# RWKV state chains in three slots a chunk, filter norms summed on TensorE, and operands of filters and convolutions prepared one unit ahead

## The chip, the core and the metric

One core of a Trainium2 chip. The metric is the device time of one execution in microseconds (us), as the median of several runs. Engines: TensorE (PE, its weight loads PEld), VectorE (DVE), ScalarE (ACT), GpSimd (POOL), and SyncE (SP), which issues most DMAs.

## The reference

A two-layer diffusion network over 1024 latent and 256 context tokens. The even layer is the one that matters here. Half of its channels go through RWKV-7 time mixing in both directions (8 heads of 64), the other 512 through an order-2 Hyena long convolution with implicit filters; both are projected from the same input and their outputs meet in one output projection. Then follow a mixture of experts, an attention layer and a second mixture.

```python
def step(s, inp):                      # RWKV, one token
    r_t, w_t, k_t, v_t, kk_t, a_t = inp
    sa = jnp.einsum('bhij,bhj->bhi', s, kk_t)
    s = s * w_t[:, :, None, :] - sa[..., None] * (kk_t * a_t)[:, :, None, :] + v_t[..., None] * k_t[:, :, None, :]
    return s, jnp.einsum('bhij,bhj->bhi', s, r_t)
...
norm = jnp.sum(jnp.abs(fwd), axis=0) + jnp.sum(jnp.abs(bwd), axis=0) + 1e-6
kc = jnp.concatenate([fwd, jnp.zeros((1, HY_ORDER, HY_WIDTH), f32), bwd], axis=0) / norm
...
z = x1 * (fft_long_conv(v, kf[:, 0]) + v * hy_b[0])
return x2 * (fft_long_conv(z, kf[:, 1]) + z * hy_b[1])
```

## The kernel before, in words

The RWKV recurrence is computed in chunks of 32 tokens, 40 steps in sequence, both directions and all heads at once; two chunks form a window whose operands are loaded together (`rw_chain`, line 873 on). A step multiplies the state S with the chunk's rows (line 914), subtracts the part from within the chunk (pA, line 900) to give the right side rh, multiplies with the inverse T of the chunk's triangular system (line 920), copies the result from PSUM into uv, next to v, which a DMA has put there (lines 890 and 926), multiplies uv with the decayed keys bt (line 932) and adds the decayed old state pr, which GpSimd makes. The outputs pY (lines 939 and 940) come from uv and the old state. The head groups are cut into two half chains (`NS = 2`), each with its own PSUM tile pc0 or pc1; the copies of uv are split by quadrant between VectorE and ScalarE. The triangular inverses are computed on VectorE per head group (`inverses`, line 810 on) and pass through DRAM.

Transforms are dense matrix products with tables in DRAM (tile tb, three buffers, loaded by GpSimd's queue). Each fp32 operand is split in a high and a low part, so that one product is three matmuls (`mm3`, lines 171 to 173). `filt` makes the Hyena filters: for two segments (context with 2 tiles of 128 rows, latent with 8), two orders and two column halves it multiplies hidden rows with weights (line 434), multiplies by a decay, takes absolute values and keeps a running sum of them on GpSimd (nacc); after the last tile a few matmuls (lines 445 and 447) sum over the rows. `filt_ctx` and `filt_lat` transform the filters and store them (kc, kl0, kl). `hy_ctx` and `hy_lat` convolve: the input's class vectors (`classvec`) times a table, products with the stored filters K (`cmul`), an inverse table product, `stage2`. Here K and the class vector of a unit are made at the head of that unit.

The order of the work: the program is written by generators that `weave` calls in turn, the one with the smaller share of its total first. On one side stand the chains and the readout (`rw_out`), on the other `fill`: the last Hyena projections (i = 3 to 11), then filters and convolutions, with steps of the layer's modulation (`ada_steps`) between. The order written is a priority: the framework's scheduler lays out the queue of every engine from its own model of durations and may put any ready instruction ahead. In the attention stage alone the queues of four engines are taken as written (line 1563).

```python
            weave(Weave(Weave.RWN, net.stage_rw(), net.rw_read()), Weave(2509, fill(net, e2, rest)))
```

## Time and profile before

| what | value |
|---|---|
| median of 3 runs | 4105.31 us (4105.16 to 4109.8) |
| the profiled execution | 4099.05 us, of it the span from first to last instruction 4097.3 us |
| mean granted TensorE clock | 0.936 |
| PE busy | 3699.7 us (90%), 30012 matmul instructions |
| VectorE, ScalarE, GpSimd busy | 2844.4 (69%), 1895.2 (46%), 976.1 us (24%) |
| the chain that ended last | PE 67%, DVE 14%, DMA 7%, issue 3%, ACT 3%, POOL 2% of the span |

Stages by the trace: input projection and RWKV preparation up to some 715 us, chains beside filters and convolutions up to 1510, output projection and first mixture up to 2480, attention up to 3440, second mixture to the end. A matmul's duration reaches from its issue to its last result and overlaps the next one, so a busy PE may still be fed slowly; the spacing of starts says how fast it is fed. An fp32 matmul counts as two instructions in the trace.

### The profile page before, as it was taken

To read this page: it belongs to the slowest core of one execution; us is meant where nothing else is said; L and a number is where in the kernel's file an instruction comes from. 1 tells how busy PE (TensorE), PEld (TensorE's weight loads), DVE (VectorE), ACT (ScalarE), POOL (GpSimd) and SP (SyncE) were. 2 spreads that over 40 slices of the span, in tenths; PEclk is the share of its full clock that TensorE was granted. 3 is DMA by queue.
4 is the path that set the end of the run, shared out by engine and by line. 5 is a ranking of instruction groups with operands and counts; after the bars stand their busy time and mean duration, and the time that the engine had idled before them with its cause. 6 is when DMAs were issued, how large, how long until landed. Compare 5 with 4: busy or idle time off the path is not lost.

```text
span 4097.3 us, 75060 instructions
## 1 busy us (share of the span) xinstructions
PE 3699.7 (90%) x30012; PEld 2928.7 (71%) x30012; DVE 2844.4 (69%) x4134; ACT 1895.2 (46%) x3037; POOL 976.1 (24%) x1098
## 2 busy tenths in 40 slices
PE   7988898789979989799999998989999796999996
PEld 4866676567758778577777776778887675777775
DVE  5478887576545774677777774167777645899997
ACT  4343443244322222266666664244444421777775
POOL 1164453333234331101111101213223111011100
PEclk8989988788989999799999999999999997999998
DMA  5244346765766875587888773345334545999996
GB/s 164 60 114 117 97 121 178 202 193 171 206 193 213 237 277 196 190 297 279 296 294 301 283 280 126 101 113 131 100 102 129 175 169 210 344 382 383 382 368 211
DMA packets 532008, 858.88 MB, mean 210 GB/s; under 512 B 161665, under 2 KB 337563, under 8 KB 527050
## 3 DMA queue, kind: packets, MB, share of 16 engines
q1 hardware_dynamic: 508704, 754.97, 55.1%
q0 software_dynamic: 19904, 90.55, 7.9%
q10 hardware_dynamic: 3050, 8.56, 0.5%
q8 instruction: 236, 3.87, 0.4%
q14 instruction: 114, 0.93, 0.1%
HBM read 708.00 MB, written 145.95 MB: 208 GB/s over the span
## 4 chain that ended last, share of the span: by engine, by line
PE 67%; DVE 14%; DMA 7%; issue 3%; ACT 3%; POOL 2%; SPq 1%; DVEq 0%; ACTq 0%; POOLq 0%
PE ps L1410 5%; PE ps L1409 5%; PE ps L1411 5%; PE pcx L1419 4%; PE pj L171 4%; PE pj L173 4%; PE pj L172 4%; PE S L1833 3%; PE py L1410 3%; PE py L1409 3%; PE py L1411 3%; DVE mx L1814 2%; PE ops L171 2%; PE ops L172 2%; PE ops L173 2%
## 5 line engine op out<-in xcount | busy, mean ns | idle before, releaser
L141 DVE TENSOR_TENSOR wrl<-wr,wrh 128x1024 fp32r<-128x1024 f32 x762 | 923.8, 1223 | 202.9 <-ACT wrh L144 170.8
L144 ACT ACTIVATE wrh<-wr 128x1024 fp32r<-128x1024 f32 x768 | 811.7, 1062 | 377.5 <-PE ps L1411 259.3
L1410 PE MATMUL ps<-wrl,xh 128*128 128x512 f32 x1024 | 410.6, 401 | 5.7 <-DVE wrl L141 5.4
L1409 PE MATMUL ps<-wrh,xh 128*128 128x512 f32 x1024 | 407.0, 399 | 2.0 <-ACT xh L144 1.4
L1411 PE MATMUL ps<-wrh,xl 128*128 128x512 f32 x1024 | 401.1, 392 | 0.0
L171 PE MATMUL pj<-hhi,whi 128*128 128x512 f32 (+3 forms) x944 | 358.5, 381 | 5.5 <-ACT qraw L144 3.2
L172 PE MATMUL pj<-hlo,whi 128*128 128x512 f32 (+3 forms) x944 | 353.0, 374 | 2.8 <-POOL hlo L141 2.4
L173 PE MATMUL pj<-hhi,wlo 128*128 128x512 f32 (+3 forms) x944 | 349.5, 371 | 1.9 <-DVE wlo L141 1.8
L1814 DVE TENSOR_REDUCE mx<-S 128x1 f32<-128x1280 f32 x128 | 185.2, 1486 | 117.8 <-PE S L1813 116.1
L1507 POOL DMA_INDIRECT x<-yo,idx x32 | 72.6, 2270 | 717.0 <-DVE yo L153 717.0
L1410 PEld LDWEIGHTS ps<-wrl,xh 128*128 128x128 f32 x1024 | 193.3, 189 | 55.3 <-DVE wrl L141 18.2
L1409 PEld LDWEIGHTS ps<-wrh,xh 128*128 128x128 f32 x1024 | 193.1, 189 | 55.1 <-issue 12.8
L1411 PEld LDWEIGHTS ps<-wrh,xl 128*128 128x128 f32 x1024 | 193.3, 189 | 37.6
L171 PEld LDWEIGHTS pj<-hhi,whi 128*128 128x128 f32 (+1 forms) x944 | 181.8, 193 | 37.9 <-issue 6.0
L1410 PE MATMUL py<-wrl,hh 128*128 128x512 f32 x512 | 206.8, 404 | 0.0
L1409 PE MATMUL py<-wrh,hh 128*128 128x512 f32 x512 | 204.4, 399 | 2.3 <-DVE yo L153 2.3
L172 PEld LDWEIGHTS pj<-hlo,whi 128*128 128x128 f32 (+1 forms) x944 | 181.9, 193 | 33.8 <-issue 4.9
L173 PEld LDWEIGHTS pj<-hhi,wlo 128*128 128x128 f32 (+1 forms) x944 | 181.2, 192 | 34.3 <-DVE wlo L141 3.8
L1411 PE MATMUL py<-wrh,hl 128*128 128x512 f32 x512 | 200.8, 392 | 0.0
L144 ACT ACTIVATE w<-S,mx 128x1280 f32<-128x1280 f32 x64 | 85.1, 1329 | 241.8 <-DVE mx L1814 241.8
L1332 POOL DMA_INDIRECT xg<-xn,idx x48 | 51.0, 1063 | 530.4 <-PE mtp L1339 477.3
L1812 PE MATMUL S<-K,Q 128*128 128x512 f32 (+1 forms) x384 | 138.0, 366 | 11.6 <-DMA Q<-qs 11.2
(439 smaller groups left out, 8833.1 us busy)
## 6 DMA issues: line engine op xcount, KB each, us to landing
wr<-in_moe_w_dram SPq DMA_DIRECT2D x384, 1024.0 KB
adaw<-in_ada_w_dram SPq DMA_DIRECT2D x160, 256.0 KB
tb<-tab_tf_dram POOLq DMA_DIRECT2D x12, 2048.0 KB, 9.5
K<-ks SPq DMA_DIRECT2D x16, 1280.0 KB
G<-G SPq DMA_DIRECT2D x72, 256.0 KB
wraw<-in_ev_w_in_dram SPq DMA_DIRECT2D x25, 512.0 KB
tb<-tab_ti_dram POOLq DMA_DIRECT2D x6, 2048.0 KB, 9.6
bt<-vts SPq DMA_DIRECT2D x80, 128.0 KB
```

What stands on the lines that cost most here:

```text
L141: return e.tensor_tensor(out, a, b, op=op)
L144: return self.s.activation(out, in_, f, **k)
L171: self.pe.matmul(ps, ah, bh, start=start and i == 0, stop=False)
L172: self.pe.matmul(ps, ah, bl, start=False, stop=False)
L173: self.pe.matmul(ps, al, bh, start=False, stop=stop and i == n - 1)
L1409: self.pe.matmul(ps[:, n], x[0], w[0][:, ns], start=k == 0, stop=False)
L1410: self.pe.matmul(ps[:, n], x[0], w[1][:, ns], start=False, stop=False)
L1411: self.last = self.pe.matmul(ps[:, n], x[1], w[0][:, ns], start=False, stop=k == 7).ins
L1419: self.behind = self.pe.matmul(out(js), x, raw[:, 256 * j:256 * j + 256], start=k == 0, stop=k == 7).ins
L1812: pe.matmul(sc[:, k0:k1], Q[:, c], K[:, c, k0:k1], start=True, stop=False)
L1814: v.tensor_reduce(mx[:, c:c + 1], sc, AX.X, OP.max, negate=True)
L1833: pe.matmul(po[:, m], wT[:, j], V[:, k + j], start=k + j == 0, stop=k + j == 9)
```

## The change

The two half chains become one over all head groups. A step has three slots, each ending in a `yield 1 / 3`: state product and right side, with the outputs of the step before behind them; T product, before which identity matmuls place v in the same PSUM tile, one copy of that tile to uv, and the next step's pA; bt product and new state. Windows are loaded one ahead (`rw_load`). The absolute values of the filters are summed over the rows by PE tile by tile into one PSUM row (`total`, one tile late), and the column form of the norm is made from that row while the next part runs (`column`). Filter weights are prepared one part ahead, class vectors and K one unit ahead. `ko` has two buffers (`KO`), the convolutions four PSUM buffers in place of three (`hyp`). Projections, transforms and readout yield in smaller pieces. Hyena projections 3 to 7 are issued ahead of the weave, 8 to 11 inside it in steps. The weave's totals become 54 and 3740, modulation steps count 6, and PE's queue follows the written order in the whole weave (`manual_schedule`).

```diff
+    def filt_weights(self, pw, o, half):
...
+        return wh, wl, dl, hb, cs
...
+        parts = [(seg, o, half) for seg in range(2) for o in range(2) for half in range(2)]
+        nxt = self.filt_weights(pw, 0, 0)
+        late = []
+        def column(seg, o, half, nr):
+            ps = pp.tile([128, 512], F32, name="fps")
+            for m in range(2):
+                self.pe.matmul(ps[:, m:m + 1], nr[:, 128 * m:128 * m + 128], self.ones[0:1, 0:1], start=True, stop=True)
+            v.reciprocal(self.fnorm[:, seg, o, 2 * half:2 * half + 2], ps[:, 0:2])
+        for n, (seg, o, half) in enumerate(parts):
...
-                        self.tt(self.g, na, na, ab[:, 0], OP.add)
...
+            wh, wl, dl, hb, cs = nxt
...
+            np_ = pp.tile([128, 256], F32, name="fnp", bufs=1)
+            prev = None
+            def total(j, ab, last):
+                self.pe.matmul(np_[0:1], self.ones[:, 0:1], ab[:, 0], start=j == 0, stop=last)
+            for j in range(nt):
...
+                ps = pp.tile([128, 512], F32, name="fps")
+                for s, w in enumerate((wh, wl)):
+                    self.pe.matmul(ps, hd[:, 128 * (j0 + j):128 * (j0 + j) + 128], w, start=s == 0, stop=s == 1)
+                if prev:
+                    total(*prev, False)
+                if late:
+                    column(*late.pop())
+                self.made = self.tt(v, Eo[:, :, j], ps.rearrange("p (d c) -> p d c", d=2), dk.unsqueeze(1).to_broadcast([128, 2, 256]), OP.mult).ins
+                ab = pw.tile([128, 2, 256], F32, name="abt")
+                if j == 0:
...
+                self.act(ab, Eo[:, :, j], AF.Abs)
+                self.tt(v, ab[:, 0], ab[:, 0], ab[:, 1], OP.max)
+                prev = j, ab
+                if j == 0 and n + 1 < len(parts):
+                    nxt = self.filt_weights(pw, *parts[n + 1][1:])
+                yield 9
+            yield 0
+            total(*prev, True)
...
+            nr = pv.tile([1, 256], F32, name="nrm", bufs=2)
+            v.tensor_scalar(nr, np_[0:1], 1e-6, None, op0=OP.add)
...
+            self.tt(v, t1, nr, hb, OP.mult)
...
+            late.append((seg, o, half, nr))
...
+            if seg:
+                for e in range(2):
+                    self.fold(Eo[:, e])
+            if half:
+                yield from (self.filt_lat if seg else self.filt_ctx)(pv, tabs, pw, pp, E, o, vec)
+            else:
+                vec = self.classvec(pv, Eo[:, 0], 0, 256) if seg else self.ctxvec(pv, Eo)
+        column(*late.pop())
...
+                vec = self.ctxvec(pv, E[1][0])
+            ko = pw.tile([128, 5, 256], F32, name="ko", bufs=KO)
...
+    def filt_lat(self, pv, tabs, pw, pp, E, o, vec):
+        units = [(cls, n, e) for cls in range(4) for n in range(2) for e in range(2)]
+        for at, (cls, n, e) in enumerate(units):
...
+            if at % 4 == 0:
+                th, tl = next(tabs)
+            if at + 1 < len(units):
+                c2, n2, e2 = units[at + 1]
+                vec = self.classvec(pv, E[n2][0][:, e2], c2, 256)
...
+                    yield 12 if cls else 6
...
+KO = 2
...
+            for k0 in (0, 4):
+                self.mm3(ps[:ncol, :n], [((wh[:, k, :ncol], wl[:, k, :ncol]), (hi[:, k, t0:t0 + n], lo[:, k, t0:t0 + n])) for k in range(k0, k0 + 4)],
+                         k0 == 0, k0 == 4)
+                if k0:
+                    evac(ps[:ncol, :n], t0, n)
+                yield 12 * n / 256
...
+                    if i == 8:
+                        yield 0
+                    yield from hyena_steps(i, bp, pt) if i >= 8 else self.at_once(hyena_steps(i, bp, pt))
...
+        self.rp = p = self.pool(es, "rw", 2, side="right")
+        q = self.pool(es, "rwq", 2, side="right")
+        pp = self.pool(es, "rwp", 1, PSUM, side="right")
+        S = q.tile([128, 2, 4, 64], F32, name="S")
+        v.memset(S, 0.0)
+        quads = self.QUADS
+        win = self.rw_load(0)
+        gv = self.rw_within(win, 0, q, pp)
+        yw, late = None, None
+        def outputs(win, i, S, uv, yw):
+            G, ar = win[1], win[0]
+            ps = pp.tile([128, 4, 64], F32, name="pY")
+            for gr in range(4):
+                for qd, h, d, qs, hs in quads:
+                    pe.matmul(ps[qs, gr], G[hs, d, gr, i, C:], uv[hs, d, gr], start=True, stop=False, tile_position=(64 * h, 32 * qd))
+                for qd, h, d, qs, hs in quads:
+                    pe.matmul(ps[qs, gr], ar[hs, d, gr, i, C:], S[hs, d, gr], start=False, stop=True, tile_position=(64 * h, 32 * qd))
+            self.act(yw[:, i], ps, AF.Copy)
+        def store(w, yw):
+            for qd, h, d, qs, hs in quads:
...
+                self.sy.dma_start(dr["y"][d, h, C * c0:C * (c0 + WIN)].rearrange("(i t) g v -> t i (g v)", t=C), yw[qs].rearrange("t i g v -> t i (g v)"))
...
+            nxt = None
+            for i in range(WIN):
+                ar, G, T, bt, vw = win
+                pr = q.tile([128, 2, 4, 64], F32, name="pr", bufs=1)
+                for d in range(2):
+                    self.tt(g, pr[:, d], S[:, d], self.dcoef[:, :, d, CS[d][w] + i].unsqueeze(2).to_broadcast([128, 4, 64]), OP.mult)
+                ps = pp.tile([128, 4, 64], F32, name="pc")
+                for gr in range(4):
+                    for qd, h, d, qs, hs in quads:
+                        pe.matmul(ps[qs, gr], ar[hs, d, gr, i, 0:C], S[hs, d, gr], start=True, stop=True, tile_position=(64 * h, 32 * qd))
+                rh = q.tile([128, 4, 64], F32, name="rh", bufs=1)
+                self.stt(v, rh, ps, -1.0, gv, OP.mult, OP.subtract)
+                if late:
+                    outputs(*late)
+                    if i == 0:
+                        store(w - 1, late[-1])
+                if i == 0:
+                    yw = p.tile([128, WIN, 4, 64], F32, name="yw", bufs=1)
+                    if w + 1 < NW:
+                        nxt = self.rw_load(w + 1)
+                yield 1 / 3
+                ps = pp.tile([128, 2, 4, 64], F32, name="pc")
+                for gr in range(4):
+                    for qd, h, d, qs, hs in quads:
+                        pe.matmul(ps[qs, 1 - d, gr], self.ident[qs, qs], vw[qs, i, gr], start=True, stop=True, tile_position=(32 * qd, 32 * qd))
+                for gr in range(4):
+                    for qd, h, d, qs, hs in quads:
+                        pe.matmul(ps[qs, d, gr], T[qs, i, gr], rh[qs, gr], start=True, stop=True, tile_position=(32 * qd, 32 * qd))
+                uv = q.tile([128, 2, 4, 64], F32, name="uv")
+                v.tensor_copy(uv, ps)
+                if i < WIN - 1:
+                    gv = self.rw_within(win, i + 1, q, pp)
+                elif nxt:
+                    gv = self.rw_within(nxt, 0, q, pp)
+                yield 1 / 3
+                ps = pp.tile([128, 2, 4, 64], F32, name="pc")
+                for d in range(2):
+                    for gr in range(4):
+                        for h in range(2):
+                            hs = slice(64 * h, 64 * h + 64)
+                            pe.matmul(ps[hs, d, gr], bt[hs, d, i, gr], uv[hs, d, gr], start=True, stop=True)
+                late = (win, i, S, uv, yw)
+                S = q.tile([128, 2, 4, 64], F32, name="S")
+                self.tt(v, S, ps, pr, OP.add)
+                yield 1 / 3
+            win = nxt
+        outputs(*late)
+        store(NW - 1, yw)
+        yield 1 / 3
+    def rw_load(self, w):
+        dr, p = self.dr, self.rp
...
+        vw = p.tile([128, WIN, 4, 64], F32, name="vw")
...
+                self.sy.dma_start(vw[r0:r0 + 32].rearrange("s i g v -> s i (g v)"),
...
+        return ar, G, T, bt, vw
...
+                if x:
+                    self.cmul(p, ps, ka, kb, yh, yl, re, im)
+                yield 3 * len(ks)
...
+        def prepare(o, cls, n):
+            K = p.tile([128, 5, W], F32, name="K", bufs=2)
+            if cls:
+                self.sy.dma_start(K[:, 0:4], self.dr["kl"][o, cls - 1, :, :, cols[n]])
+            else:
+                self.sy.dma_start(K, self.dr["kl0"][o, :, :, cols[n]])
+            return (K,) + self.classvec(p, us[n], cls, W)
+        units = [(o, cls, n) for o in range(2) for cls in (0, 2, 1, 3) for n in range(2)]
+        for u in us:
+            self.fold(u)
+        ready = [prepare(*units[0])]
...
+                    K, hi, lo = ready.pop()
...
+                    at = units.index((o, cls, n)) + 1
+                    if n == 0:
+                        ready.append(prepare(*units[at]))
...
+                if cls != 3:
+                    ready.append(prepare(*units[at]))
...
+                for n, (acc, (yh, yl)) in enumerate(zip(accs, ys)):
...
+                            if x:
+                                self.stage2(cls, av[:, m], ps[:, 0], ps[:, 1], pw, W)
+                            yield 12 if cls else 6
+                    if cls != 3:
+                        continue
+                    if o == 0:
+                        u = self.hu.tile([128, 8, W], F32, name="ul")
+                        self.sy.dma_start(u, self.dr["hv"][1, NC:, cols[n]].rearrange("(b p) c -> p b c", p=128))
+                        self.tt(self.v, u, acc, u, OP.mult)
+                        us[n] = u
+                        self.fold(u)
+                        if n == 0:
+                            ready.append(prepare(1, 0, 0))
...
-    RWN = 64
+    RWN = 54
+    FILL = 3740
...
+        def parts():
+            with ExitStack() as e2:
+                yield from net.filters(tabs, net.pool(e2, "fillp", 3, PSUM))
+            with ExitStack() as e2:
+                yield from net.stage_hy(tabs, net.pool(e2, "hyp", 4, PSUM))
+        for w in parts():
...
+                done += 6
+                w += 6
...
-            weave(Weave(Weave.RWN, net.stage_rw(), net.rw_read()), Weave(2509, fill(net, e2, rest)))
+            next(rest)
+            with tc.manual_schedule(engines={mybir.EngineType.PE}):
+                weave(Weave(Weave.RWN, net.stage_rw(), net.rw_read()), Weave(Weave.FILL, fill(net, e2, rest)))
...
```

## Rows read from the trace of the kernel before

**Rows 1.** The page of the profile: its first line.

```profile
span 4097.3 us, 75060 instructions
```

**Rows 2.** Stretches: length, PE, PEld, DVE, ACT, POOL busy, clock, DMA share, GB/s.

```profile
710.00:790.00 80.00, 53.94 (x1047) 38.90 (x1045) 46.05 (x118) 20.77 (x53) 25.22 (x39) 0.66 0.78 209
...
1105.00:1210.00 105.00, 73.83 (x1614) 60.60 (x1606) 42.39 (x99) 19.37 (x52) 31.78 (x54) 0.85 0.79 227
...
1350.00:1510.00 160.00, 148.59 (x1072) 122.37 (x1070) 123.20 (x208) 40.80 (x77) 61.11 (x78) 0.97 0.79 251
710.00:1510.00 800.00, 697.20 (x10912) 562.15 (x10910) 498.47 (x1031) 259.40 (x582) 288.60 (x415) 0.90 0.70 207
```

**Rows 3.** Tiles pc and hps: ns min/median/max, first and last start us.

```profile
L920 PE MATMUL pc<-rh,T x1280: 212/214/312, 715.0 to 1332.0; 32*32 32x64 f32 x183
...
L173 PE MATMUL hps<-tb,yl x128: 277/280/388, 1158.5 to 1506.4; 128*128 128x256 f32 x128
```

**Rows 4.** Timeline of PE from 1040 and 1076 us: start, length, instruction.

```profile
1040.21 0.68 PE L932 MATMUL pc<-uv,bt 64*64 64x64 f32 x16
1040.82 0.34 PE L939 MATMUL pY<-uv,G 64*32 64x64 f32 x8
...
1075.95 0.43 PE L914 MATMUL pc<-S,arw 64*32 64x64 f32 x16
1076.31 0.39 PE L171 MATMUL fpk<-vh,tb 128*128 128x256 f32 x1
1076.53 0.28 PE L172 MATMUL fpk<-vl,tb 128*128 128x256 f32 x1
...
1078.06 0.28 PE L173 MATMUL fpk<-vh,tb 128*128 128x256 f32 x1
1078.27 0.42 PE L914 MATMUL pc<-S,arw 64*32 64x64 f32 x14
```

**Rows 5.** Chain of waits, PE pieces: start, length, line, instructions.

```profile
1399.54 0.86 PE rps L992 x2
...
1670.36 3.34 PE adaps L268 x64
```

**Rows 6.** Chain of waits, 1095 to 1290 us: two loads.

```profile
1140.47 9.28 DMA ul<-hv
...
1257.40 10.67 DMA K<-kl
```

**Rows 7.** Groups by shape, 680 to 1490 us: busy us, mean ns, idle.

```profile
L926 DVE COPY uv<-pc 32x128 f32<-32x128 f32 x160 | 44.1, 281 | 47.3 <-PE pc L920 30.4 <-ACT uv L144 12.3 <-PE pA L900 1.4
L144 ACT ACTIVATE uv<-pc 32x128 f32<-32x128 f32 x160 | 41.7, 268 | 97.6 <-DVE uv L926 95.5
...
L141 DVE TENSOR_TENSOR S<-pc,pr 128x256 f32<-128x256 f32 x80 | 33.3, 420 | 54.1 <-PE pc L932 53.3
...
L153 DVE SCALAR_TENSOR_TENSOR rh<-pc,gv 128x128 f32<-128x128 f32 x80 | 21.6, 283 | 19.3 <-PE pc L914 16.8 <-ACT yw L144 1.4 <-ACT gv L144 0.8
```

**Rows 8.** Groups by shape, 680 to 1490 us: convolution and filter operations.

```profile
L141 DVE TENSOR_TENSOR cm<-hps,K 128x512 f32<-128x512 f32 x75 | 47.9, 681 | 27.2 <-PE hps L173 23.4 <-DMA K<-kc 2.6 <-POOL cy L141 0.9
...
L141 DVE TENSOR_TENSOR EO<-fps,dk 128x512 f32<-128x512 f32 x40 | 27.1, 685 | 8.0 <-PE fps L434 6.6 <-ACT dk L144 0.6 <-ACT abt L144 0.4
...
L144 ACT ACTIVATE abt<-EO 128x512 f32<-128x512 f32 x40 | 25.0, 625 | 20.1 <-POOL nacc L141 14.6 <-POOL EO L439 3.1 <-DVE EO L141 2.0
...
L141 DVE TENSOR_TENSOR abt<-abt 128x256 f32<-128x256 f32 x40 | 21.3, 536 | 6.7 <-ACT abt L144 6.5
```

**Rows 9.** Timeline of VectorE, 671 to 700 us: first and last mix.

```profile
672.43 0.96 DVE L599 TENSOR_SCALAR u<-raw,pcol 128x1312 f32<-128x1312 f32 x1
673.44 1.58 DVE L153 SCALAR_TENSOR_TENSOR u<-raw,pcol,u 128x1312 f32<-128x1312 f32 x1
...
696.75 0.96 DVE L599 TENSOR_SCALAR u<-raw,pcol 128x1312 f32<-128x1312 f32 x1 [1.43 <-ACT raw L144]
```

**Rows 10.** Attention stage, one stretch, columns as in rows 2.

```profile
2720.00:3140.00 420.00, 406.24 (x2501) 345.47 (x2500) 311.69 (x415) 200.06 (x404) 115.35 (x84) 1.00 0.40 107
```

More of the change, by code (lines that the diff above doesn't have):

```diff
@@ L553, in norm_T, with proj, proj_steps @@
                 self.split(hi[:, k, o:o + w], lo[:, k, o:o + w], t[:, :w], ehi=self.v, elo=self.g if k % 2 else self.v)
[L555 removed]
+    def proj(self, *args):
+        for _ in self.proj_steps(*args):
+            pass
+    def proj_steps(self, w_src, ncol, hi, lo, wp, pp, toks, evac):
         raw = wp.tile([128, 8, 128], F32, name="wraw", bufs=1)
@@ L625, in stage_a2, with run, run_steps @@
         self.sy.dma_start(g2, a["rw_g2"][0])
-        def run(c0, ncol, out, w0, w1, w2, b=None):
+        def run(*args):
+            for _ in run_steps(*args):
+                pass
+        def run_steps(c0, ncol, out, w0, w1, w2, b=None):
             raw = rp.tile([128, GG + 2], F32, name="raw")
@@ L857, in stage_rw @@
             yield from self.rw_chains(es)
+    QUADS = [(qd, qd // 2, qd % 2, slice(32 * qd, 32 * qd + 32), slice(64 * (qd // 2), 64 * (qd // 2) + 64)) for qd in range(4)]
     def rw_chains(self, es):
-        a, v, g = self.a, self.v, self.g
+        v, g, pe, dr = self.v, self.g, self.pe, self.dr
         self.dram("y", [2, 2, GG, 4, 64])
-        self.rp = self.pool(es, "rw", 2, side="right")
-        self.rq = q = self.pool(es, "rwq", 2, side="right")
-        self.rps = self.pool(es, "rwp", 1, PSUM, side="right")
@@ L945, in rw_chain, with rw_within @@
-        for qd, h, d, qs, hs in quads:
-            c0 = CS[d][w]
-            self.sy.dma_start(dr["y"][d, h, C * c0:C * (c0 + WIN)].rearrange("(i t) g v -> t i (g v)", t=C), yw[qs].rearrange("t i g v -> t i (g v)"))
-        yield 1
-        return st
+        return ar, G, T, bt, vw
+    def rw_within(self, win, i, q, pp):
+        G, vw = win[1], win[4]
+        ps = pp.tile([128, 4, 64], F32, name="pA")
+        for gr in range(4):
+            for qd, h, d, qs, hs in self.QUADS:
+                ms = slice(64 * h + 32 * (1 - d), 64 * h + 32 * (1 - d) + 32)
+                self.pe.matmul(ps[qs, gr], G[ms, d, gr, i, 0:C], vw[ms, i, gr], start=True, stop=True, tile_position=(ms.start, 32 * qd))
+        gv = q.tile([128, 4, 64], F32, name="gv")
+        self.act(gv, ps, AF.Copy)
+        return gv
@@ L2018, in fill @@
         done, at = 0, 0
-        for w in chain(net.filters(tabs, pp), net.stage_hy(tabs, pp)):
+        def parts():
[4 more added lines that the diff above has]
+        for w in parts():
             done += w
```

271 lines of the change are left out of this document (79 added, 192 removed).

## The prediction, made before the change was run

> **What bounds the kernel now.** Only the stage in which the RWKV state chains run beside the Hyena filters and convolutions is edited, so I read the span [rows 1] and then a table of that stage by stretches [rows 2]. The reader is to see that from 710 to 1510 us no engine is full: TensorE (PE) is busy for 697 of 800 us, but its granted clock is 0.90, so part of the time it ran at 1.2 instead of 2.4 GHz; VectorE has 498, ScalarE 259. Two stretches are poor: 710 to 790 (PE 54 of 80 at 0.66), where the filters start cold, and 1105 to 1210 (74 of 105 at 0.85), where the convolutions do.
>
> The stage's ends come from tile views [rows 3]: the first matmul on an inverse T starts at 715.0, the last convolution matmul at 1506.4, 791 us later. What PE needs of that I price by spacing, since durations overlap. In a timeline of PE [rows 4] thirteen 256-column matmuls take 1078.06 - 1076.53 us, 0.118 each. Sixteen small ones take 0.36 us up to the next start, and a change of kind costs 0.1 us going in (0.21 against 0.118) and 0.1 coming out (0.22): 0.2 us a visit, and (0.36 - 0.1) / 16 = 0.0165 us a small instruction; of the 64 x 64 kind (16 in 0.61 us) 0.0325. An fp32 instruction of 512 columns takes 0.43 us, and 64 modulation ones 3.34 us [rows 5].
>
> A chain step before: 160 x 0.0165 + 32 x 0.0325 + 8 visits x 0.2 = 5.3 us; 40 steps, 211. Transforms: 768 (filters) and 1536 (convolutions) x 0.118 = 271. Filter products 80 x 0.235 = 19; norms 4; modulation 512 / 64 x 3.34 = 27; readout (36 fp32 pairs, 160 turned tiles) 43; Nyquist rows 6. Sum 581 of 791 us: 73% of the time PE is fed, the rest is waiting and half clock. The chain of waits names part of it: loads asked for in the unit that needs them, ul 9.3 and K 10.7 us [rows 6].
>
> **The change part by part.**
>
> *Chains.* VectorE per step before: 4 x 0.281 + 2 x 0.283 + 2 x 0.420 = 2.53 us [rows 7]. After: the right side at 128 x 256, 0.42 (nearest: S at that size); a 128 x 512 copy out of PSUM and a 128 x 512 sum, 0.68 each (nearest: cm) [rows 8]: 1.78. That is 30 us less in 40 steps, and ScalarE loses 160 x 0.268 = 43. Neither is the bound, so both count as nothing; they shorten queues. PE gets 32 identity instructions a step, but visits fall from eight to three: 192 x 0.0165 + 1.04 + 0.6 = 4.8 us, 193 in 40 steps. The pr products on GpSimd have as many elements and two slots to land.
> ScalarE's copies waited for VectorE's by 95.5 us in sum [rows 7], and that goes. VectorE alone now makes the hop in 0.68 us instead of a pair's 0.56: 0.12 us, 5 us in 40 steps if bare; the fill covers it, so nothing is counted. The Trainium skill (TensorEngine Tiling (Array Packing), PSUM Bottleneck) wants both ScalarE and VectorE on PSUM's evacuation, which speaks against this part; by it the sum would be those 5 us worse.
>
> *Norms on PE.* 40 one-row fp32 products of 256 columns, two instructions each, 0.43 us: 17 instead of 4 (bounds 0.24, the single-pass spacing, and 0.86: 10 to 34 us). GpSimd's running sums go. New wait: tile j-1's product stands behind tile j's matmuls and needs the product, Abs and max of j-1, 0.69 + 0.63 + 0.54 us [rows 8] plus queueing, some 3 us against a period of about 2.2. Behind it stand fill and chain. I take 0.8 us x 40 = 32 (0 to 1.2: 0 to 48).
>
> *Hyena projections 8 to 11* follow the chain's first slots on PE, with their weight loads and row stores on SP. Before they ran during the last group's inverses; three of their mixes lie inside that computation on VectorE, 0.96 + 2 x 1.58 = 4.1 us each [rows 9]. T then comes up to 13 us earlier: start 702 (bounds 702 and 715). In return PE gets 4 x 24 x 5 x 0.118 = 56 us inside the stage. What waits for the projections' memory, the hd and table loads on GpSimd's queue among it, starts after them, 90 us later than before; the chain goes on meanwhile.
>
> *One unit ahead.* K loads and class vectors are issued a unit of 24 matmuls (2.8 us plus a chain slot) before use, so the K waits go. Late next at the two starts are the loads that do not move: filter weights with GpSimd's sums and the split; uc, the context's K, ul. SP carries the same bytes; the chain's windows are asked for about two steps ahead. PSUM for the convolutions goes from 3 to 4 buffers, ko from 1 to 2: no cost. Per start I take 18 us of idle PE, 36 in all (the second lost 105 - 74 = 31 before, one load is 8 or more: 16 to 62).
>
> *Written order on PE.* The attention stage is the nearest row with one: PE busy 406 of 420 us, clock 1.00, with VectorE at 312, 74% [rows 10]. But there the other engines are written out too. A slot here is followed by 3740 / 54 / 3 = 23 units, 2.7 us, and by up to 1.1 us of other chain work, against 0.2 us for the last matmul [rows 3] and 0.42 to 0.68 for the evacuation; a free VectorE is covered, a queue on it only in part. I take 0.4 us x 120 slots = 48 (0 to 1.3, two 0.68 us operations in front: 0 to 156). First loads: 5.
>
> Sum of PE work: 193 + 271 + 19 + 17 + 27 + 56 + 43 + 6 = 632. Idle: 48 + 32 + 36 + 5 = 121. 753 us from 702 on ends at 1455 instead of 1506: 51 us earlier. What follows only shifts. The profiled execution took 4099.05 us around a span of 4097.3; it becomes 4048. The median of the runs shown stands 6.3 us above it: I forecast 4054.
>
> **The rivals.**
>
> *Blocked at the head (slower).* A late operand holds all that is written behind it, where before other work could stand in front. Place: the 120 slots. It decides from 0.4 + 51 / 120 = 0.83 us of waiting a slot; two operations in front make 1.3, 108 us more: 4162. For it: VectorE is busy 123 of 160 us from 1350 to 1510 [rows 2], and its order stays with the scheduler. Against: attention bears 74% with PE full. The Trainium skill (TensorE: Matmul & The Clock Gate, Step-by-step: what each phase is for) says that matmuls stay in program order and only weight loads are pulled ahead, the condition of this rival; no run so far shows it alone.
>
> *Fed like attention.* PE's busy share times clock is 0.97 there and 0.87 x 0.90 = 0.78 here, where 73% is work; in proportion 0.97 means 91%. 632 / 0.91 = 695, end 1397, 109 us earlier: 3996. For it: shorter evacuations, loads ahead. Against: the two starts.
>
> *Given back.* The start stays at 715 (+13), both starts lose 31 us (+26), the norm waits are 1.1 us (+12): 4105. The projections and norms moved onto PE inside the stage then eat the gain. That they move is sure; that the starts improve isn't.
>
> **How the numbers follow.** Forecast 0.40, fed like attention 0.26, blocked 0.20, given back 0.14. The predicted time is the forecast's, 4054. With one term at its bound it lies between 4006 (no slot waits) and 4162. The range 3985 to 4135 takes in the fed case and the nearer half of the blocked one; an almost perfect feed and slots above 1.1 us stay outside. About 0.2%, 8 us, is what a measurement of this kernel tells from no change. Faster: 0.40 + 0.26 and a little of the rest, 0.67; same 0.12; slower 0.21.
>
> **What would show it.** Right: the first T matmul near 702, the last convolution matmul near 1455, the stage's clock above 0.95, chain steps some 14 us apart, PE waiting for VectorE in small pieces. Wrong: the T start unmoved; PE idle by more than 0.83 us a slot (blocked) or more than 1.2 us a filter tile before its norm product; starts that lose over 31 us; or a gain outside this stage, which nothing here explains.

## The result and the profile after

The changed kernel takes 4164.93 us (median; 4162.0 to 4172.03) where the kernel before took 4107.35 in the same comparison: ratio 1.0143, interval 1.0125 to 1.016. It is 58 us slower; 4054 was forecast, and the range ended at 4135.

Line numbers are those of the changed kernel from here on. The tile views of pc and hps after, which answer to [rows 3] (ns min/median/max, first and last start in us):

```profile
L975 PE MATMUL pc<-rh,T x1280: 211/214/312, 699.3 to 1362.3; 32*32 32x64 f32 x183
...
L173 PE MATMUL hps<-tb,yl x128: 274/281/416, 1202.1 to 1569.2; 128*128 128x256 f32 x128
```

The first T product comes at 699.3, 16 us earlier than before, the last convolution product at 1569.2, 63 us later. The span is 62.9 us longer (4160.2 against 4097.3): all of it arises in this stage, which takes 870 us where it took 791.

The table of stretches after, which answers to [rows 2] (length, then PE, PEld, DVE, ACT, POOL busy, clock, DMA share, GB/s):

```profile
650.00:700.00 50.00, 28.12 (x251) 19.74 (x249) 29.49 (x75) 10.61 (x21) 4.44 (x10) 0.60 0.74 203
...
700.00:850.00 150.00, 120.12 (x2284) 93.35 (x2284) 70.45 (x132) 30.27 (x59) 33.35 (x47) 0.85 0.58 161
850.00:1140.00 290.00, 248.57 (x5292) 191.17 (x5292) 176.56 (x296) 111.16 (x215) 49.11 (x58) 0.91 0.65 189
1140.00:1260.00 120.00, 72.00 (x1518) 62.75 (x1518) 51.84 (x87) 19.30 (x37) 37.88 (x50) 0.79 0.66 197
1260.00:1380.00 120.00, 104.35 (x2380) 94.80 (x2378) 63.90 (x122) 20.16 (x42) 47.34 (x62) 0.94 0.72 218
1380.00:1570.00 190.00, 165.37 (x1019) 137.83 (x1018) 124.95 (x205) 40.98 (x75) 62.73 (x78) 0.87 0.59 186
```

Busy time times granted clock, stretch by stretch from 700 us, is the work that TensorE did at full clock: 102 + 226 + 57 + 98 + 144 = 627 us. Idle are 870 - 710 = 160 us, and 710 - 627 = 83 us were lost to half clock. (A stretch's clock counts its idle time too; in 87 windows of 10 us the same sum gives 645, 160 and 65.) The last row of [rows 2] gives 697.2 x 0.90 = 627 us of work before, 103 idle, 70 lost to half clock (in 80 windows of 10 us 638, 103 and 59). So TensorE has about as much to do in the stage as before; it waits 57 us more and loses 6 to 13 more to the clock.

What the waits are, from the view of waits of PE (total us, times, longest), first 700 to 1380, then 1380 to 1570 us:

```profile
PE fnp L446 <- DVE abt L141: 44.2, 23, 5.9
PE hps L171 <- ACT vh L144: 38.2, 3, 21.3
PE fps L453 <- ACT fwh L144: 11.3, 1, 11.3
...
PE pA L1026 <- issue: 6.8, 3, 2.6
...
PE pc L988 <- DVE uv L977: 4.5, 3, 3.1
...
PE pc L972 <- DVE rh L153: 1.5, 1, 1.5
PE pc L957 <- DVE S L141: 1.4, 2, 1.2
```

```profile
PE rps L1089 <- DVE rrs L1081: 11.0, 3, 4.3
PE hps L171 <- ACT vh L144: 4.7, 1, 4.7
PE rpv L1078 <- ACT yb L144: 4.7, 5, 2.1
```

The chain's own slots (lines 957 to 988, and pA) wait 15 us in 120 slots. The long waits are of the fill: norm products, class vectors at the convolutions' start, the first filter weights, the readout's reciprocals (rrs) and squares (yb) at the end.

The longest, 21.3 us, is best read on VectorE. Its timeline there (start, length, instruction, idle before it and its releaser):

```profile
1204.42 0.48 DVE L153 SCALAR_TENSOR_TENSOR x2c<-hps,fscale,x2c 128x256 f32<-128x256 f32 x1 [0.84 <-PE hps L173]
...
1214.89 0.48 DVE L153 SCALAR_TENSOR_TENSOR x2c<-hps,fscale,x2c 128x256 f32<-128x256 f32 x1 [3.16 <-DMA x2c<-hx]
1227.55 0.48 DVE L153 SCALAR_TENSOR_TENSOR x2c<-hps,fscale,x2c 128x256 f32<-128x256 f32 x1 [12.18 <-DMA x2c<-hx]
1231.86 0.48 DVE L153 SCALAR_TENSOR_TENSOR x2c<-hps,fscale,x2c 128x256 f32<-128x256 f32 x1 [3.82 <-DMA x2c<-hx]
1234.15 0.69 DVE L141 TENSOR_TENSOR vt<-ul 128x512 f32<-128x512 f32 x1 [1.81 <-DMA yT<-x2c]
```

Four outputs of the context's convolution go through one buffer, tile x2c, which the class vectors' temporary vt shares: each load waits until the store before it has landed (three waits on SP's queue, 11.7 us together), and the first latent class vector waits for all four. TensorE is behind that:

```profile
1215.00:1235.00 20.00, 1.17 (x6) 0.88 (x5) 2.16 (x5) 0.00 (x0) 0.76 (x1) 0.50 0.56 190
```

In these 20 us it works 1.2 us, at half clock. The four loads stood in one buffer before as well, and in the kernel before's chain of waits, the view of [rows 6], two of them can be read:

```profile
1173.28 4.64 DMA x2c<-hx
...
1200.32 3.20 DMA x2c<-hx
```

### The profile page after: what moved, and what is told of

It reads as the page before. It is cut to its first block, busy times and chain, and to the rows that moved or that the text cites. A ratio compares the mean times of both kernels' runs of the same rounds, so it can differ in the third digit from the quotient of the medians.

```text
span 4160.2 us, 77110 instructions
## 1 busy us (share of the span) xinstructions
PE 3680.5 (88%) x31356; PEld 2914.1 (70%) x31356; DVE 2821.3 (68%) x3933; ACT 1853.8 (45%) x2877; POOL 916.8 (22%) x970
## 4 chain that ended last, share of the span: by engine, by line
PE 53%; DVE 7%; DMA 2%; ACT 2%; issue 2%; SPq 0%; POOL 0%; DVEq 0%; ACTq 0%; POOLq 0%
PE ps L1502 5%; PE ps L1501 5%; PE ps L1503 5%; PE pcx L1511 4%; PE S L1925 3%; PE py L1502 3%; PE py L1501 3%; PE py L1503 3%; PE pj L173 2%; PE pj L171 2%; PE pj L172 2%; DVE mx L1906 2%; PE ops L171 2%; PE ops L172 2%; PE ops L173 2%
## 5 line engine op out<-in xcount | busy, mean ns | idle before, releaser
L1904 PE MATMUL S<-K,Q 128*128 128x512 f32 (+1 forms) x384 | 138.0, 366 | 11.3 <-DMA Q<-qs 10.8
```

The costliest lines, as they stand in the source:

```text
L1904: pe.matmul(sc[:, k0:k1], Q[:, c], K[:, c, k0:k1], start=True, stop=False)
```

## The experiments

Ratios are to the kernel before, run beside them; the changed kernel's is 1.0143. "T" and "end" are the first T product and the last convolution product of the profiled execution.

| run | TensorE's order | ratio (interval) | T, end (us) |
|---|---|---|---|
| free | free | 0.9992 (0.9979 to 1.0006) | 712.0, 1481.2 |
| gps | written | 1.0139 (1.012 to 1.0158) | 700.0, 1573.6 |
| late2 | written | 1.0103 (1.0085 to 1.0121) | 706.2, 1565.4 |
| defer | written | 1.0153 (1.0129 to 1.0176) | 700.3, 1572.9 |
| x2c | written | 1.0077 (1.0056 to 1.0099) | 693.3, 1532.3 |
| starts | written | 1.0069 (1.0052 to 1.0086) | 701.0, 1542.6 |
| defer_starts_holes | written | 1.0108 (1.0087 to 1.0128) | 702.5, 1556.8 |
| proj | written | 1.0085 (1.0065 to 1.0106) | 776.3, 1549.0 |
| proj_x2c | written | 1.0079 (1.0059 to 1.0099) | 773.2, 1527.3 |
| head | free up to the filters | 1.0086 (1.0064 to 1.0108) | 713.4, 1549.7 |
| mid | free, filters to end of chain | 1.0033 (1.0019 to 1.0046) | 701.3, 1523.9 |
| tail | free after the chain | 1.0056 (1.0038 to 1.0074) | 700.9, 1525.6 |
| headtail_x2c | written, filters to end of chain | 0.9957 (0.9939 to 0.9974) | 717.9, 1485.0 |
| before_x2c | free (kernel before) | 0.995 (0.9934 to 0.9967) | 714.5, 1484.6 |
| free_x2c | free | 0.9916 (0.99 to 0.9933) | 714.3, 1474.1 |
| free_x2c_again | free | 0.994 (0.9924 to 0.9957) | 717.7, 1465.5 |
| free_starts | free | 0.9936 (0.9912 to 0.996) | 711.9, 1466.4 |
| free_x2c_fwq | free | 0.9913 (0.9899 to 0.9928) | 718.1, 1464.1 |

**The written order undone.**

```diff
-            with tc.manual_schedule(engines={mybir.EngineType.PE}):
-                weave(...)
+            weave(...)
```

> Edit: the changed kernel with TensorE's order in the chains' stage left to the scheduler again, all else as changed. Theory (heads): in written order TensorE stands behind a few late operands (57 us before norm products, 43 before class vectors, 11 before filter weights in the profile after) and runs at 1.2 GHz after each, while chain work written behind could have run; let free, the stage loses at least half of its 160 idle us: 4060 to 4100. Rival 1 (late whatever the order): what the heads wait for is late itself and the chain has nothing ready: 4150 to 4175. Rival 2 (the order is what carries the three-slot chain): without it chain slots come in the wrong places and the readout ends late: over 4180.

Ratio 0.9992, 4096.68 us: 62 us (1.5% of the time before) come back with this one edit. The written order costs as much as the whole loss, and the rest of the change is worth nothing that can be measured in the time. The time is the theory's; the idle time fell from 160 to 110 us, less than the half that it asked for. The stretches of this run, as above:

```profile
650.00:710.00 60.00, 57.26 (x513) 47.20 (x513) 42.91 (x87) 14.46 (x29) 5.85 (x16) 0.96 0.65 185
...
1230.00:1480.00 250.00, 237.49 (x2976) 208.33 (x2975) 178.03 (x312) 59.02 (x112) 107.46 (x136) 0.96 0.68 210
710.00:1480.00 770.00, 660.49 (x12139) 542.18 (x12139) 469.85 (x825) 215.03 (x418) 228.71 (x287) 0.90 0.70 206
```

TensorE is all but full from 650 to 710 us: the scheduler puts the Hyena projections there by itself, though the program offers them later (their products, tile pj, are busy for 35.3 us from 650 to 700; in the changed kernel for 3.3). The stage then holds 660 x 0.90 = 594 us of work instead of 627. Its end is 25 us ahead of the kernel before, but the output projection's first product waits 18.6 us for its operand there (PE ops <- ACT yh, 1492 to 1510), so the gain is partly given back behind the stage.

PE's waits in this run, from 710 to 1480 us:

```profile
PE pA L1026 <- DMA G<-G: 29.4, 10, 7.2
PE pc L972 <- DVE rh L153: 21.8, 5, 8.7
...
PE hps L171 <- ACT vh L144: 3.8, 2, 2.2
...
PE fnp L446 <- DVE abt L141: 3.6, 4, 1.4
...
PE fps L453 <- ACT fwh L144: 1.3, 1, 1.3
```

Before norm products TensorE now stands 3.6 us instead of 44.2, before class vectors 3.8 instead of 38.2, before the first filter weights 1.3 instead of 11.3: ready work went in front of them. Of the 110 idle us that are left some 80 stand before the chain's own products (pA, pc, pY), where it was 15 in written order.

**The norms.** Three runs change only how the filter norm gets to TensorE: summed on GpSimd as before (gps), each product two tiles late (late2), the last product of a group and what follows it written behind work of the next group (defer).

```diff
 gps
-                if prev:
-                    total(*prev, False)
...
+                self.tt(self.g, na, na, ab[:, 0], OP.add)
 late2
-                if prev:
-                    total(*prev, False)
+                if len(prev) == 2:
+                    total(*prev.pop(0), False)
 defer
+                if end and j == 1:
+                    end()
...
```

> Edit: the changed kernel with the filter norm summed on GpSimd again and one product a filter group; PE order written. Theory (heads): 32 of 40 one-row products go (32 x 0.43 = 14 us) and their waits with them (about 1.1 us each, 35), and some of the half clock behind them: 4105 to 4125. Rival (the wait moves): the one product left stands behind GpSimd's last sum, later than VectorE's maximum by 0.7 us and more, and the products that went were hidden in waits: 4150 to 4170.

> Edit: the changed kernel with each norm product written two tiles behind its tile in place of one, with a third buffer for the maxima. Theory (heads): the waits before norm products inside the loops (18 of 23, 27 us, in 860 to 1140) go, those at a group's end and in the two-tile context groups stay: 20 to 35 us less, 4130 to 4145. Rival (the tiles' pace): VectorE, ScalarE and three PSUM buffers set the pace of the loops, and TensorE waits for the same before the next tile's matmuls: within 8 us of 4165.

> Edit: the changed kernel; a filter group's last norm product, its bias tap, folds and first class vector are written behind the next group's second tile or behind the first unit of transforms, where that unit needs only the group before. Theory (heads): the waits at the eight group ends (26 us in five visits in the run with GpSimd's sum were 45 in eight) are exposed because nothing is written between a group's last tile and its product: 20 to 35 us less, ratio 1.006 to 1.010. Rival (VectorE's chain of product, Abs, maximum is late in each tile): as changed, 1.013 to 1.015, with the waits moved onto fnp inside the loops or fps.

The waits of PE before norm products, from 700 to 1380 us, in gps and in defer:

```profile
PE fnp L448 <- POOL nacc L141: 44.8, 8, 9.0
```

```profile
PE fnp L445 <- DVE abt L141: 32.4, 15, 6.4
...
PE fpk L171 <- ACT vh L144: 8.7, 4, 3.4
...
PE hps L172 <- DVE vl L141: 7.0, 2, 6.3
```

With GpSimd's sum eight waits cost what 23 cost with the products on TensorE: 44.8 against 44.2 us, and the time does not move. That is the rival's forecast: in written order the sums that left GpSimd were no gain and no loss. In the kernel before the same sum on GpSimd made TensorE wait a tenth of that (710 to 1510 us, line 445 of that kernel):

```profile
PE fps L445 <- POOL nacc L141: 4.8, 4, 1.8
```

With TensorE's products in free order it was 3.6. So it is the order, and not the engine that sums, that makes these waits long. Written later (defer), 12 us of the waits go and some 15 come up before class vectors, which took 1 in the changed kernel: the time is about the rival's, the place, for which it named fnp and fps, is not. In late2 the waits fell to 39.6 us and the median by 19 us, to 4145.77: more than the rival's 8 us, and 1 us short of the theory's range. Its interval (to 1.0121) ends just below the changed kernel's (from 1.0125). Its profiled execution, the slowest of its four, ends the stage only 4 us earlier, so where the 19 us came from is not shown. None of the three gets more than 19 us there.

**The convolutions' start.** The x2c loads are asked for at the start, each into a slice of acc, which is idle then (x2c); in starts uc lies there too, and the ul loads, folds and first class vectors go out during the context's convolution.

```diff
+        x2c = self.hu.tile([128, 8, W], F32, name="x2c", tag="acc")
+        for ch in range(4):
+            self.sy.dma_start(x2c[:, ch], self.dr["hx2"][ch, :, 0:NC])
...
-                        x2 = p.tile([128, NC], F32, name="x2c", tag="vt")
-                        self.sy.dma_start(x2, self.dr["hx2"][ch, :, 0:NC])
+                        x2 = x2c[:, ch]
```

> Edit: the changed kernel, the four x2c loads of the context's output asked for at the start of the convolutions into a slice each of a tile that is idle then, where they went one after the other through one buffer. Theory (heads): the empty stretch from 1217 to 1237 us is VectorE standing in three x2c waits in a row (19 us) with the latent class vectors behind it and TensorE's written order behind those; it goes, with the half clock after it: 25 to 35 us less, 4130 to 4140. Rival (transfers): the DMA engines are full there (0.94 to 1.00 from 1205 to 1225 us), and earlier loads only push back uc, K and the chain's window: within 8 us of 4165.

> Edit: the changed kernel; uc and x2c lie in the slots of acc, so that the x2c loads, both ul loads, their folds and the first latent class vectors go out during the context's convolution; the uc loads themselves stay. PE order written. Theory (heads): besides the 33 us of x2c alone the second wait before a latent class vector (8 to 10 us) goes, with half clock behind it, the 10 us before uc stay: 40 to 50 us under the changed kernel, ratio to before 1.002 to 1.005. Rival (transfers): 2 MB more asked for in the context's 60 us delay K and the chain's windows: no better than x2c alone, 1.006 to 1.010.

> Edit: the changed kernel with TensorE's order free and the x2c loads early. Theory (heads): the x2c wait cost 33 us because chain work stood behind it in written order; in free order the chain runs on meanwhile, so the same edit gives under 10 us: 4088 to 4097, ratio 0.997 to 1.000. Rival (supply): the convolutions themselves were late by that much, so 20 to 30 us less here too: 4066 to 4077.

> Edit: the kernel before with only the x2c loads early. Theory (supply): the four loads through one buffer held the convolutions in the kernel before too (VectorE waits 11 us for them, the first latent class vector comes 44 us after the first x2c product), so the edit gives 20 to 30 us without any part of the change: ratio 0.992 to 0.995. Rival: before, the chain ran on meanwhile and its slower steps set the end, so it gives under 8 us: ratio over 0.998.

PE's waits for class vectors from 700 to 1380 us, in x2c and in starts, there with the next line:

```profile
PE hps L171 <- ACT vh L144: 18.9, 3, 9.9
```

```profile
PE hps L171 <- ACT vh L144: 10.8, 1, 10.8
PE adaps L275 <- ACT adart L144: 10.7, 8, 6.3
```

The x2c edit gives 27 to 33 us with written order, as expected. But it gives 21 us in the kernel before and 21 to 31 with free order (0.9992 to 0.994 and 0.9916). So my theory, that this wait is dear because the written order holds chain work behind it, falls: it was late whatever the order, and in the kernel before too. It belongs to the 105 - 74 = 31 us that the second start lost before [rows 2]: in the same stretch, 1105 to 1210 us, before_x2c has TensorE busy for 85.4 us at a clock of 0.91, where it was 73.8 at 0.85. In starts the second wait at this start, 4.3 us, goes (x2c's line also counts one of 4.7 us that lies behind 1380 us in starts) and another (adaps, 6.3) takes its place; it is no better than x2c alone, as the rival said.

**The pieces together, with empty fill.** 70 units without work stand where the first loads are asked for, so that chain slots are written there.

```diff
+        yield 70
...
-    FILL = 3740
+    FILL = 3880
```

> Edit: both of the above, and 70 units of empty fill (three chain slots) written where the filters and the convolutions ask for their first loads, FILL 3740 to 3880. Theory (heads): the gains add (45 and 25) and the two load waits of 11 and 10 us are covered by chain slots (10 to 15 more): 80 to 85 us under the changed kernel, 4075 to 4085, ratio 0.993 to 0.996, faster than before. Rival (the supply runs out): with the heads gone the pace is set by VectorE and the transfers, and the stage ends no sooner than the free order's 1481: 4095 to 4105.

Ratio 1.0108, worse than starts alone; both forecasts missed. The waits before filter weights went, but modulation products then stood 21.9 us in six waits for their weights. In a written order an idle stretch that is filled at one place comes up at the next operand.

**The hole ahead of T.** From 650 to 700 us TensorE is busy 28 us at a clock of 0.60 after the change. Its timeline shows what it stands at:

```profile
682.93 0.65 PE L972 MATMUL pc<-vw,ident 32*32 32x64 f32 x32
683.51 0.66 PE L726 MATMUL vtp<-ident,u 128*128 128x128 f32 x4
686.74 1.11 PE L726 MATMUL vtp<-ident,u 128*128 128x128 f32 x4 [2.57 <-ACT vts L144]
...
699.35 0.42 PE L975 MATMUL pc<-rh,T 32*32 32x64 f32 x2 [5.14 <-DMA T<-xt]
```

The second slot's T product is written ahead of most of projections 8 to 11, and T is the last thing to arrive. The run proj issues these projections ahead of the written stage again; proj_x2c adds the early loads.

```diff
-                    if i == 8:
-                        yield 0
-                    yield from hyena_steps(i, bp, pt) if i >= 8 else self.at_once(hyena_steps(i, bp, pt))
+                    self.at_once(hyena_steps(i, bp, pt))
+                yield 0
...
-    FILL = 3740
+    FILL = 3236
```

> Edit: the changed kernel with Hyena projections 8 to 11 issued ahead of the written stage again, as before; FILL 3740 to 3236 for the 504 units that leave it; the rest as changed. Theory (the move): between 660 and 700 us, while the last inverse group is awaited, TensorE was busy 20 of 40 us at a clock of 0.63 after the change and 40 of 40 near full before; the projections filled that hole for nothing and now cost 56 us behind it. Back in the hole they give 56 less the 13 by which T comes later: 35 to 45 us less, 4115 to 4125, ratio 1.003 to 1.006. Rival (slots): the loss is in the order of chain slots against filters, and fewer units of fill between slots (20 against 23) expose more of it: under 15 us gained, ratio over 1.010.

> Edit: the same with the x2c loads early. Theory (two holes, independent): the gains add, 33 and 40: ratio 0.995 to 0.998. Rival (one bound behind both): the second gain is mostly lost: ratio 1.000 to 1.005.

Ratio 1.0085: 24 us, less than the theory and more than the rival. T now starts at 776.3, though with free order it started at 712.0. A timeline of PE and VectorE's groups from 741 to 775 us, both of proj, say why:

```profile
774.51 1.01 PE L446 MATMUL fnp<-abt,ones 128*1 128x256 f32 x2 [32.66 <-DVE abt L141]
```

```profile
L141 DVE TENSOR_TENSOR N<-N,Xt 128x30 f32<-128x30 f32 (+14 forms) x30 | 10.9, 363 | 1.0
L141 DVE TENSOR_TENSOR Xt<-N 128x30 f32<-128x30 f32 (+14 forms) x30 | 10.8, 362 | 14.5 <-DMA fw<-in_hy_f_w_dram 13.5
```

VectorE works on the last inverses (22 us, after 14 us of waiting for a load), the filters' first maximum is behind them, the first norm product waits 32.7 us for that, and the T product is written behind the norm product. The chain started 64 us later than free order had it start. In the medians the early loads then gave next to nothing (1.0079), though the stage of the profiled execution ended 22 us earlier; how far the two gains add stays unclear.

**Stretch by stretch.** Three runs free the order in one stretch each; the last joins the first and third to the early loads.

```diff
+            for free, until in ((HEAD, lambda: units.done >= 504), (MID, lambda: len(chain.gens) < 2), (TAIL, lambda: False)):
+                with ExitStack() as e3:
+                    if not free:
+                        e3.enter_context(tc.manual_schedule(engines={mybir.EngineType.PE}))
+                    weave(chain, units, until=until)
```

> Edit: TensorE's order left to the scheduler until the Hyena projections are through (504 units of fill), written from there on. Theory (sum of small pieces): counted by stretch, TensorE loses 33 of 50 us from 650 to 700 us in the changed kernel (idle 22, half clock 11) and 5 of 60 with free order; with this stretch free the projections go into the hole and 15 to 28 us come back: ratio 1.007 to 1.011. Rival (one place): the loss sits in the filters and convolutions and what is gained here is lost again at the filters' first product: ratio over 1.012.

> Edit: TensorE's order free from the end of the projections to the end of the chain, written before and after. Theory (sum of small pieces): the filters' start, loops, convolutions' start and the rest up to 1377 us lose about 37 + 59 + 58 + 20 us in written order; with chain work free to fill them a part comes back: 25 to 40 us, ratio 1.004 to 1.008. Rival (one place): this stretch holds all the chain slots, and with it all 68 us that the free order gives: ratio under 1.002.

> Edit: TensorE's order free from the end of the chain on (readout beside convolutions), written before. Theory (sum of small pieces): from 1380 to 1570 us the written order loses 44 of 190 us (readout products behind ScalarE's squares and VectorE's square roots, class vectors), the free order 21 of its last 250; 15 to 30 us come back: ratio 1.007 to 1.011. Rival (one place): only chain slots matter, and there are none here: ratio over 1.012.

> Edit: written order only from the end of the projections to the end of the chain, free before and after, and the x2c loads early. Theory (sum of small pieces): 1.0143 less 33 us for x2c, 20 for the head and 20 for the tail: ratio 0.995 to 0.998, above the wholly free order with early x2c (0.9916). Rival (written order helps where the chain is): under 0.9916, better than the free one.

Freed alone, the head gives 0.57% (23 us), the middle 1.10% (45), the tail 0.87% (36), where all three together give 1.51% (62). So it is no one place; each stretch costs, and what one gains is partly waited for in the next. Middle and tail gave somewhat more than expected, and the tail has no chain slot; from 1380 us to the end it reads

```profile
1380.00:1526.00 146.00, 139.48 (x958) 116.60 (x956) 119.47 (x197) 39.83 (x72) 59.61 (x74) 0.96 0.70 215
```

against 165 of 190 us at 0.87 with the written order: 25 us of idle time and 22 of half clock became 7 and 6 (61 of the stretch's 1019 instructions come ahead of 1380 us there). In written order the readout's products stood behind ScalarE's squares and VectorE's reciprocals of ScalarE's square roots (line 1081), in waits of up to 4.3 us; freed, PE's waits in the stretch come to 6 us, so other products were ready. With a written middle alone and early loads, 0.9957 is above the wholly free 0.9916, as the theory of pieces said; from the repeat of that kernel, 0.994, it can't be told.

**A version ahead of both.** free_starts puts the early class vectors into the free order; the last two runs repeat the free order with early x2c loads and then ask for the filters' first loads on ScalarE's queue.

```diff
-        nxt = self.filt_weights(pw, 0, 0)
+        nxt = self.filt_weights(pw, 0, 0, self.s)
```

> Edit: the changed kernel with TensorE's order free, uc and x2c in acc's slots and the ul loads, folds and first class vectors during the context's convolution. Theory (supply): the second wait before a class vector goes with the first: 5 to 12 us under the free order with early x2c alone, ratio 0.988 to 0.991. Rival: VectorE's queue takes the folds earlier and holds chain steps: ratio 0.991 to 0.994.

> The free order with the early x2c loads once more, in five rounds beside the next kernel. Theory: 0.990 to 0.993 again, faster than both kernels. Rival (the spread of 4058 to 4078 us that such kernels show lies about a slower middle): 0.993 to 0.997.

> Edit: the same, with the filters' first weights, decay rates, bias and time column asked for on ScalarE's queue, which is idle there, where SP's queue comes to them at 737 us, behind 16 loads of the last inverse group (723 to 737). Theory (supply, again): the filters' first product moves from 748 to about 730 us and 8 to 17 us come back: 4050 to 4060, ratio 0.987 to 0.990. Rival: from 740 to 776 us VectorE works on the last inverses, and TensorE's chain waits for it (9 us before one slot); the filters' first products wait there too: within 4 us of the other.

free_starts does not differ from the free order with early loads (0.9936 against 0.994 and 0.9916); its rival's range holds it. The repeat, 0.994, lies in its rival's range too, 10 us above the first run of the same kernel. The other queue brings the filters' first product from 752.4 to 735.3 us, tile fwh in the one and the other:

```profile
L453 PE MATMUL fps<-fwh,hd x3: 628/793/797, 752.4 to 770.1; 128*128 128x512 f32 x3
```

```profile
L454 PE MATMUL fps<-fwh,hd x3: 397/794/796, 735.3 to 748.7; 128*128 128x512 f32 x3
```

That is 17 us, of which 8 are left in the time beside the repeat: 4066.85 us against 4074.57. The ratio, 0.9913 (0.9899 to 0.9928), is the lowest here and above the range of the theory; from the first run of free_x2c, 0.9916, it can't be told. The Trainium skill (Trainium Kernel Development and Optimization, Key Constraints) says that a second issuing engine saves only the issue time; the trace agrees, since what went is the turn behind 16 loads on SP's queue (727 to 741 us in the repeat, in which that queue waits for 1.1 us in all): the first filter load is issued at 718.3 instead of 742.1 us.

## Why the prediction was wrong

Its terms against the profile after:

| term (us) | forecast | measured |
|---|---|---|
| first T product | 702 | 699.3 |
| PE work from there | 632 | 627 |
| chain slots | 48 | 15 |
| norm waits | 32 | 44 |
| the two starts | 36 | 50 (11.3 + 38.2) |
| first loads and the rest | 5 | 51 |
| half clock | 0 | 83 (65 by windows of 10 us) |
| stage | 753 | 870 |

- **The start and the work** came out as worked out. For the work that is partly luck: the same prices gave 581 us before, where rows give 627, so the prices were low by some 46 us and the change saves about that much more than I counted.
- **Half clock** is the term of the sum that failed most: 83 us (65 by windows of 10 us, with 645 of work) of the 117 by which the stage is longer than forecast. The sum added work at full clock and idle time and nothing for the clock, and "the stage's clock above 0.95" stood among the signs of being right, though the row of before said 0.90 [rows 2], 70 us in 800. Most of it was there before, so leaving it out made the forecast too short, but it is not what made the changed kernel slower. After long waits the next products ran at half clock: 1.2 us of work at 0.50 from 1215 to 1235 us, 28 us at 0.60 from 650 to 700.
- **Written order** was priced at the wrong place, and its cost is what makes the changed kernel slower; without it (0.9992) the forecast gain isn't there either, since TensorE then idles 110 us in the stage where it idled 103 before. I looked for its waits in the 120 chain slots and allowed 0.4 us each; they took 0.12. The order's cost is at the fill's own operands (norm products, class vectors, filter weights, readout) with ready work behind them, which the run with free order and the three stretch runs show: 62 us in all, with the waits before norm products falling from 44.2 to 3.6 us and before class vectors from 38.2 to 3.8. The attention stage [rows 10] was the wrong comparison, as the prediction itself said against it: there the other engines are written out too.
- **The starts**: 50 us of idle time where 36 were taken. "Late next at the two starts are the loads that do not move" was right in kind, but the list named filter weights, uc, K and ul and missed x2c, the one that set the second start. I priced a load that was removed (K) without reading which wait ended last there; the wait for x2c was in the profile of before, in the view that gave [rows 6].
- **Norms**: 1.1 us a tile for 0.8, a term of 32 that measured 44; undoing it changes nothing (1.0139), since in written order GpSimd's sum made TensorE wait as long (44.8, against 4.8 in the kernel before).
- **The rest**: of its 51 us some 21 are waits of the readout (rps, rpv) and 13 of the modulation (adaps), for which the sum had no term.
- **Projections** were booked as 56 us more in the stage against a T 13 us earlier. That makes 43 us of loss which the forecast expected to win back from idle time, and it did not; the 56 was not measured by itself (with free order, which is through with them by 711 us, the stage holds 33 us less work).
- **The rivals**: "blocked at the head" gave 4162 and the measured time is 4165, but its place, the slots with a deciding 0.83 us, was not where it happened. So the agreement of its number is luck. In kind, a late operand that holds ready work behind it, it was right, and it had a chance of 0.20. "Given back" had the sizes of the norm waits (1.1) but not of the T start.
- **Copies on VectorE alone**, priced at 5 us if bare: TensorE waited 4.5 us for uv at line 988 in all, so they decide nothing. The Trainium skill (TensorEngine Tiling (Array Packing), PSUM Bottleneck) wants both ScalarE and VectorE on PSUM's evacuation; no run here splits these copies, so that is not tested.

Not tried: the kernel before with its old chain in written order, and the three-slot chain without the prepared operands. Of the change without the written order only the sum is known, 0.9992; with early x2c loads it stands at 0.9916 and 0.994, and the kernel before with the same loads at 0.995.

## What to carry to other kernels

Before fixing an engine's order by hand, go through every operand that it will stand at, not only those of the critical chain, and ask what ready work is written behind it; the scheduler had been filling those holes here for nothing (4.8 us before norm products in the kernel before, 44 in written order). Take the stage's granted clock into the sum as time lost, beside idle time, and expect a long new hole to cost again in clock. At the start of a stage read which wait ends last before pricing the loads that a change moves: four loads through one shared buffer held this one, before and after.

## What was not expected of the hardware

Waits cost again in clock, but by no fixed share: in the tail 25 us of idle time, in waits of at most 4.7 us, came with 22 us lost at half clock, and both went together (7 and 6) when the order was freed; from 850 to 1140 us 41 us of idle time came with 22; and this stretch of the changed kernel stood 2.3 of 10 us at full clock:

```profile
960.00:970.00 10.00, 7.74 (x233) 6.86 (x227) 3.80 (x7) 3.65 (x8) 0.64 (x1) 1.00 1.05 322
```

And one buffer for load, product and store costs a round trip each time: the x2c products came 10.5, 12.7 and 4.3 us apart, for 0.48 us of work each.
